# Delta-rule scan with forward and backward products in alternation, gathered in two bursts a step

## The chip, the cores and the metric

The kernel runs on one core of a Trainium2 chip. The metric is the device time of one execution in microseconds; the median of three runs before the change is 1783.05 us (1782.53 to 1787.27). The engines are named as the profile names them: PE (TensorE, with PEld for its weight loads), DVE (VectorE), ACT (ScalarE), POOL (GpSimd) and SP (SyncE, which here only issues DMAs).

## What is computed

One layer of an encoder on 1024 tokens of width 1024, all in fp32: a norm and a wide input projection; grouped attention; a gated delta rule that runs over the sequence forward and backward; gates and an output projection; then 16 experts that each choose 128 tokens. The change lies in the delta rule. With 8 heads of 64 and chunks of 64 tokens, each direction is a loop over 16 chunks (cut from the reference):

```python
def step(state, inp):
    u_n, w_n, a_n, qg_n, kd_n, gl_n = inp
    v_new = u_n - w_n @ state
    o_n = qg_n @ state + a_n @ v_new
    state = state * gl_n[..., None, None] + jnp.einsum('bhck,bhcv->bhkv', kd_n, v_new)
    return state, o_n
```

`w` and `u` hold the inverse of a 64x64 unit triangular matrix, one for each chunk, head and direction. `gl` is one decay a head and chunk, and `beta` and another decay scale the rows of `v_new`.

## The kernel before

Before the scan, the projections of q, k and v are normed and convolved (`dn_group`), the gates become scalars (`dn_gates`, `dn_scalars`), and `dn_tile` writes the masked products of each chunk to DRAM. `dn_invert` inverts only the two 32x32 blocks on the diagonal of each triangular matrix, on VectorE, and writes them to DRAM (`w_d`). The block beside the diagonal is made in the scan, by `scan_merge`: minus the product of the lower inverse, the block between them (`n_d`) and the upper inverse, as two rounds of 32x32 products, 8 heads for each direction.

The scan runs both directions at once. Step t works on chunk t forward and on chunk 15 - t backward. As t and 15 - t are one even and one odd, one chunk's 64 tokens lie on partitions 0 to 63 and the other's on 64 to 127 of the same tiles, and so in different row blocks of the PE array. A step consists of

- `pk` (L626): keys and queries times the state, 4 products of 128x128 for each direction; DVE scales them (L629) and takes them from v, which gives x (L633)
- `pv` (L638): the inverse times x, 8 products of 64x64 for each direction, all in one array block; DVE scales the result by the scalars `bs` to `vb` and `va` (L643, L644)
- `pu` (L653): the state's update, 8 products of 64x64 for each direction, whose outputs alternate between two column blocks; DVE adds it to the state, which was scaled by `gls` (L648, L655), and ACT copies the state into the form that `pk` reads (L658)
- `po` (L663): the output, 8 products of 64x64 for each direction, added into O (L669 to L672).

An fp32 product is two pairs of weight load and matmul, so a line with 8 products for each direction has 32 loads a step. `scan_merge` for step t + 1 (L604 to L613) has twice as many: 32 loads in its first round (L606), 32 in its second (L612). `scan_load` (L587 to L594) issues the ten DMAs of the next step on SP's queue.

The scan leaves PE room, and `late_fill` puts the rest of the input projection there: 15 groups of 48 matmuls of 128x512 (L1147). `scan` writes the order down: so many fills between the parts of a step (`FILL`), pieces of the attention's preparation (`attn_prep`, in the first eight steps; its transposes are L143), pieces of the output's norm (`scan_post`) and of the modulation (`mod_step`, L901, L903). This written order is a priority and not the final one: a planner with a cost model goes through the program and gives each engine, one instruction at a time, the first one in written order whose inputs it expects to be ready. The engine's queues then keep that order. PSUM tiles come in three kinds: "pj" for the fills, and "dn" and "tr" with two buffers each.

The scalars `gls` (for each step and head) and `bs` (for each step, row and head) are put in the order of the steps before the scan, by 32 and 64 copies on POOL (L430, L452, L453). POOL's queue also issues the weight loads of the projection (L269).

Of the kernel before, what the change touches and what calls it, by code (L numbers as in the profile page):

```python
# [7 lines left out]
F = mybir.dt.float32  # L8
# [24 lines left out]
FILL = 12, 10, 4, 4, 8, 48  # L33
# [40 lines left out]
def rev(ap):  # L74

    *dims, (step, n) = [list(x) for x in ap.ap]
    return bass.AP(tensor=ap.tensor, offset=ap.offset + step * (n - 1), ap=dims + [[-step, n]])


class K:  # L80
# [274 lines left out]
    def dn_gates(self, ps):  # L355
# [71 lines left out]
        for t in range(16):  # L427
            for d in range(2):
                n = t if d == 0 else 15 - t
                nc.gpsimd.tensor_copy(gls[:, t, d * 4:d * 4 + 4], gl[:, n // 2, n % 2, d * 4:d * 4 + 4])  # L430
        self.eg, self.gls, self.dk = eg, gls, dk

    def dn_scalars(self):
# [13 lines left out]
        for t in range(16):  # L447
            for d in range(2):
                n = t if d == 0 else 15 - t
                j, x = divmod(n, 2)  # L450
                rows = slice(64 * x, 64 * x + 64)
                nc.gpsimd.tensor_copy(bs[rows, t, 0, :], b2[rows, j, d, :])  # L452
                nc.gpsimd.tensor_copy(bs[rows, t, 1, :], b2d[rows, j, d, :])  # L453
# [119 lines left out]
    def scan_load(self, t):  # L573


        nc = self.nc
# [3 lines left out]
        for d in range(2):  # L580
            n = t if d == 0 else 15 - t
            x = n % 2
            r = slice(64 * x, 64 * x + 64)
            src = self.w_d[d].rearrange("(n h) (b s c) -> n b s h c", h=8, b=2, s=32)
            nsrc = self.n_d[d, n].rearrange("h (b s) (e c) -> b s h e c", b=2, e=2)
# [3 lines left out]
            nc.sync.dma_start(nf[f], nsrc[d, :, :, 1 - d, :])  # L589
            quads.append((f, o, slice(32 * d, 32 * d + 32), slice(32 - 32 * d, 64 - 32 * d)))  # L590
            nc.sync.dma_start(at[r].rearrange("p h c -> p (h c)"), self.a_d[d, n // 2, r])
            nc.sync.dma_start(kv[r], self.kv_d[n // 2, r])
            k = self.kqs[d][:, t % 2]
            nc.sync.dma_start(k, self.kq_d[n])  # L594
            kq.append(k)
        return w, at, kv, kq, nf, quads

    def scan_merge(self, ops):
# [4 lines left out]
        for f, o, cf, co in quads:  # L603
            nc.vector.transpose(wt[f], w[f, :, cf])  # L604
            for h in range(8):
                nc.tensor.matmul(pq[o, h], nf[f, h], wt[f, h], start=True, stop=True, skip_group_check=True)  # L606
            nc.scalar.activation(pt[o], pq[o], AF.Copy, scale=-1.0)
        yield
        pr = self.pa.tile([128, 8, 32], F, name="tr", bufs=2)
        for f, o, cf, co in quads:  # L610
            for h in range(8):
                nc.tensor.matmul(pr[f, h], pt[o, h], w[o, h, co], start=True, stop=True, skip_group_check=True)  # L612
            nc.scalar.copy(w[f, :, co], pr[f])  # L613

    def scan_step(self, t, ops):
# [20 lines left out]
        for r in rs:  # L636
            for h in range(8):
                nc.tensor.matmul(pv[r, h], w[r, h], x[r, h], start=True, stop=True, skip_group_check=True)  # L638
# [20 lines left out]
        yield  # L659
        po = self.pa.tile([128, 8, 64], F, name="dn", bufs=2)  # L660
        for d in range(2):
            for h in range(8):
# [250 lines left out]
    def scan(self, late, ak, sta):  # L913
# [23 lines left out]
        fill(FILL[5])  # L937
        for _ in self.scan_merge(ops):
            fill(6)
        for t in range(16):  # L940
            nxt = self.scan_load(t + 1) if t < 15 else None
            step = self.scan_step(t, ops)
            next(step)
            for _ in cur:
                pass
# [18 lines left out]
            fill(FILL[4])  # L964
# [660 lines left out]
```

## Time and profile before

| | |
|---|---|
| median of three runs | 1783.05 us |
| the profiled execution | 1782.9 us |
| its span (first to last instruction) | 1780.7 us |
| mean granted TensorE clock | 0.965 of full |
| PE busy | 1663.8 us (93%) |
| DVE busy | 1453.2 us (82%) |
| ACT busy | 924.4 us (52%) |
| POOL busy | 256.7 us (14%) |

Busy times are unions of an engine's instructions over the span; for PE the ends of matmuls are modelled and overlap, so weight loads (PEld) show its pace better. The scan's first state product stands at 412.8 us and its last at 747.0 us. Several small tiles share a buffer and stand under its name: the n blocks (`nf`) and their partner `wt` under Sc, and x, `va`, `vb` under st. In a group of the profile, the number behind the bar is the busy time, then the mean of one instruction, then the idle time of the engine just before them and what ended it.

### The profile page before, as it was taken

To read this page: it belongs to the slowest core of one execution; us is meant where nothing else is said; L and a number is where in the kernel's file an instruction comes from. 1 tells how busy PE (TensorE), PEld (TensorE's weight loads), DVE (VectorE), ACT (ScalarE), POOL (GpSimd) and SP (SyncE) were. 2 spreads that over 40 slices of the span, in tenths; PEclk is the share of its full clock that TensorE was granted. 3 is DMA by queue.
4 is the path that set the end of the run, shared out by engine and by line. 5 is a ranking of instruction groups with operands and counts; after the bars stand their busy time and mean duration, and the time that the engine had idled before them with its cause. 6 is when DMAs were issued, how large, how long until landed. Compare 5 with 4: busy or idle time off the path is not lost. (4 is left out here: it accounts for less than half of the span.)

```text
span 1780.7 us, 28660 instructions
## 1 busy us (share of the span) xinstructions
PE 1663.8 (93%) x10363; PEld 1333.4 (75%) x10363; DVE 1453.2 (82%) x2523; ACT 924.4 (52%) x1372; POOL 256.7 (14%) x287
## 2 busy tenths in 40 slices
PE   6999998389999999999999999939999999999997
PEld 4777876377887778778887778827777777777776
DVE  6899895965777667679998366889999999999997
ACT  5654522113332422268884133327777777777775
POOL 0041512021111100021111212220000110010000
PEclk8999999699999999899999999969999999999999
DMA  9466389256667775431114454569999999999991
GB/s 272 124 178 178 108 214 212 71 174 166 192 188 180 206 224 134 137 124 34 34 35 160 159 204 155 191 238 309 387 387 383 370 384 385 382 373 379 387 335 24
DMA packets 283053, 390.81 MB, mean 219 GB/s; under 512 B 78299, under 2 KB 151695, under 8 KB 282655
## 3 DMA queue, kind: packets, MB, share of 16 engines
q1 hardware_dynamic: 247103, 328.15, 55.5%
q0 software_dynamic: 12960, 47.19, 9.7%
q10 hardware_dynamic: 22848, 13.63, 2.7%
q8 instruction: 82, 1.34, 0.3%
q14 instruction: 60, 0.49, 0.1%
HBM read 330.14 MB, written 58.77 MB: 218 GB/s over the span
## 5 line engine op out<-in xcount | busy, mean ns | idle before, releaser
L1514 DVE TENSOR_TENSOR ew<-er,ew 128x1024 fp32r<-128x1024 f32 x384 | 452.2, 1219 | 30.1 <-ACT ew L1513 30.1
L1513 ACT CAST ew<-er 128x1024 fp32r<-128x1024 f32 x384 | 391.1, 1049 | 138.2 <-PE pj L1567 103.0
L1567 PE MATMUL pj<-ew,xT 128*128 128x512 f32 x1536 | 368.0, 396 | 4.5 <-DVE ew L1514 4.5
L1567 PEld LDWEIGHTS pj<-ew,xT 128*128 128x128 f32 x1536 | 283.3, 188 | 76.4 <-DVE ew L1514 19.5
L1584 PE MATMUL tr<-ew,aT 128*128 128x512 f32 x768 | 191.3, 398 | 0.0
L1584 PEld LDWEIGHTS tr<-ew,aT 128*128 128x128 f32 x768 | 139.7, 188 | 30.5 <-DVE ew L1514 3.5
L279 PE MATMUL pj<-hTh,wl 128*128 128x512 f32 (+1 forms) x368 | 118.6, 401 | 26.4 <-DVE wl L273 26.4
L279 PE MATMUL pj<-hTh,wh 128*128 128x512 f32 (+1 forms) x368 | 118.5, 402 | 3.6 <-ACT hTh L252 1.8
L279 PE MATMUL pj<-hTl,wh 128*128 128x512 f32 (+1 forms) x368 | 118.6, 399 | 1.4 <-DVE hTl L255 1.4
L272 ACT CAST wh<-wraw 128x1024 fp32r<-128x1024 f32 (+1 forms) x45 | 46.7, 1037 | 137.3 <-PE pj L279 66.5
L279 PEld LDWEIGHTS pj<-hTh,wl 128*128 128x128 f32 (+1 forms) x368 | 69.3, 189 | 43.5 <-DVE wl L273 27.0
L1590 POOL DMA_INDIRECT out_dram<-xe,idxT x16 | 37.1, 2317 | 405.6 <-DVE tok L1488 351.1
L269 POOL DMA_DIRECT2D wraw<-in_w_in_dram x42 | 37.7, 898 | 369.4 <-DVE wl L273 278.7
L834 DVE TENSOR_REDUCE am<-pj 128x1 f32<-128x1024 f32 x64 | 77.8, 1217 | 12.4 <-PE pj L829 11.8
L1193 PE MATMUL pj<-hTh,uw 128*128 128x512 f32 x256 | 83.5, 404 | 1.0 <-DVE uth L1199 0.5
L279 PEld LDWEIGHTS pj<-hTh,wh 128*128 128x128 f32 (+1 forms) x368 | 68.6, 190 | 19.8 <-ACT hTh L252 1.9
L1147 PE MATMUL pj<-hTh,wh 128*128 128x512 f32 x240 | 82.7, 412 | 0.0
L1147 PE MATMUL pj<-hTh,wl 128*128 128x512 f32 x240 | 81.9, 410 | 0.0
L279 PEld LDWEIGHTS pj<-hTl,wh 128*128 128x128 f32 (+1 forms) x368 | 68.7, 188 | 17.6 <-DVE hTl L255 2.0
L1147 PE MATMUL pj<-hTl,wh 128*128 128x512 f32 x240 | 81.3, 409 | 0.0
L836 ACT ACTIVATE ap<-pj,am 128x1024 f32<-128x1024 f32 x64 | 71.9, 1123 | 13.9 <-DVE am L834 8.5
L829 PE MATMUL pj<-kT,qT 128*128 128x512 f32 x256 | 77.0, 412 | 1.5 <-ACT ap L836 1.5
(373 smaller groups left out, 3144.5 us busy)
## 6 DMA issues: line engine op xcount, KB each, us to landing
er<-in_w_gate_dram SPq DMA_DIRECT2D x128, 512.0 KB, 7.2
er<-in_w_up_dram SPq DMA_DIRECT2D x128, 512.0 KB
er<-in_w_down_dram SPq DMA_DIRECT2D x128, 512.0 KB, 10.0
wraw<-in_w_in_dram POOLq DMA_DIRECT2D x42, 512.0 KB, 5.8
mw<-in_w_ada_dram SPq DMA_DIRECT2D x64, 256.0 KB, 3.6
wt<-in_w_ada_dram SPq DMA_DIRECT2D x16, 512.0 KB, 8.6
gate_d<-y ACTq DMA_DIRECT2D x32, 256.0 KB, 3.3
kv<-kv_d SPq DMA_DIRECT2D x32, 256.0 KB, 3.6
```

The lines of the kernel that those rows point to most:

```text
L269: (queue or nc.gpsimd).dma_start(raw[:, :, :n], self.i["w_in"][0, :, col:col + n].rearrange("(k p) c -> p k c", p=128))
L272: nc.scalar.copy(wh[:, :, :n], raw[:, :, :n])
L279: self.nc.tensor.matmul(ps[q][:n], w[:, k, :n], x[k][:, q * 512:(q + 1) * 512], start=(k == 0 and w is wh and x is self.hTh), stop=(k == 7 ...
L829: nc.tensor.matmul(ps[:, kh], qT[:, i * 128:(i + 1) * 128], self.kT[a][:, s, kh * 512:(kh + 1) * 512], start=(s == 0), stop=(s == 1), skip ...
L834: nc.vector.reduce_max(m, ps, axis=AX.X, negate=True)
L836: nc.scalar.activation(p, ps, AF.Exp, bias=m, scale=1.0, accum_out=self.rv[:, h, half * 4 + i:half * 4 + i + 1])
L1147: nc.tensor.matmul(ps[q], a[:, k], x[k][:, q * 512:(q + 1) * 512], start=(k == 0 and a is wh and x is self.hTh), stop=(k == 7 and a is wl))
L1193: nc.tensor.matmul(ps, w[:, k], v[k][:, qs], start=(k == 0 and p == 0), stop=(k == 3 and p == 2))
L1513: nc.scalar.copy(hi, raw)
L1514: nc.vector.tensor_sub(lo, raw, hi.bitcast(F))
L1567: nc.tensor.matmul(pg[m], x[:, 2 * kp + k], wi[:, k], start=(kp == 0 and k == 0 and n == 0), stop=(kp == 3 and k == 1 and n == 2))
L1584: nc.tensor.matmul(py[q], x[:, k], wi[:, q], start=(k == 0 and n == 0), stop=(k == 7 and n == 2))
```

## The change

Six edits, all of order but the last:

1. In `scan_merge`, `pv`, `pu` and `po` the loop over heads is now the outer one and that over directions the inner, so that successive products belong to different directions. In `pu` each direction has a tile of its own, one "dn" and one "tr".
2. In `scan_merge` the evacuations of a round (L607, L613) come behind the products of both directions.
3. `scan_step` loses a yield: `pu` and `po` are written as one piece.
4. In `scan` the next step's merge starts before `pv`, and its second round follows `po`. The fills between are 12, 10, 8 and 8, where they were 12, 10, 4, 4 and 8.
5. `scan_load` issues the W and n blocks of both directions first, then kqs, kv and sa.
6. `gls` is filled by 2 copies on ACT and `bs` by 8, with strides over the steps and, for the backward direction, a negative one (`rev1`).

```diff
-FILL = 12, 10, 4, 4, 8, 48
+FILL = 12, 10, 8, 8, 48
...
+def rev1(ap):
+    part, (step, n), *dims = [list(x) for x in ap.ap]
+    return bass.AP(tensor=ap.tensor, offset=ap.offset + step * (n - 1), ap=[part, [-step, n], *dims])
...
-        for t in range(16):
-            for d in range(2):
-                n = t if d == 0 else 15 - t
-                nc.gpsimd.tensor_copy(gls[:, t, d * 4:d * 4 + 4], gl[:, n // 2, n % 2, d * 4:d * 4 + 4])
+        gl = gl.rearrange("p j x e -> p (j x) e")
+        for d, turn in ((0, lambda a: a), (1, rev1)):
+            nc.scalar.copy(gls[:, :, d * 4:d * 4 + 4], turn(gl[:, :, d * 4:d * 4 + 4]))
...
-                nc.gpsimd.tensor_copy(bs[rows, t, 0, :], b2[rows, j, d, :])
-                nc.gpsimd.tensor_copy(bs[rows, t, 1, :], b2d[rows, j, d, :])
+        for x in range(2):
+            rows = slice(64 * x, 64 * x + 64)
+            for s, b in enumerate((b2, b2d)):
+                nc.scalar.copy(bs[rows, x::2, s, :], b[rows, :, 0, :])
+                nc.scalar.copy(bs[rows, 1 - x::2, s, :], rev1(b[rows, :, 1, :]))
...
             nc.vector.transpose(wt[f], w[f, :, cf])
-            for h in range(8):
+        for h in range(8):
+            for f, o, cf, co in quads:
                 nc.tensor.matmul(pq[o, h], nf[f, h], wt[f, h], start=True, stop=True, skip_group_check=True)
+        for f, o, cf, co in quads:
             nc.scalar.activation(pt[o], pq[o], AF.Copy, scale=-1.0)
...
-        for r in rs:
-            for h in range(8):
+        for h in range(8):
+            for r in rs:
                 nc.tensor.matmul(pv[r, h], w[r, h], x[r, h], start=True, stop=True, skip_group_check=True)
...
-            for d, r in enumerate(rs):
-                pu = self.pa.tile([128, 4, 64], F, name="dn", bufs=2)
-                for h in range(8):
-                    hb = 64 * (h % 2)
-                    nc.tensor.matmul(pu[hb:hb + 64, h // 2], kv[r, 0, h * 64:h * 64 + 64], vb[r, h],
+            pu = [self.pa.tile([128, 4, 64], F, name=n, bufs=2) for n in ("dn", "tr")]
+            for h in range(8):
+                hr = slice(64 * (h % 2), 64 * (h % 2) + 64)
+                for d, r in enumerate(rs):
+                    nc.tensor.matmul(pu[d][hr, h // 2], kv[r, 0, h * 64:h * 64 + 64], vb[r, h],
                                      start=True, stop=True, skip_group_check=True)
-                nc.vector.tensor_add(self.Sc[:, d * 4:d * 4 + 4], sg[:, d * 4:d * 4 + 4], pu)
+            for d in range(2):
+                nc.vector.tensor_add(self.Sc[:, d * 4:d * 4 + 4], sg[:, d * 4:d * 4 + 4], pu[d])
...
-        yield
         po = self.pa.tile([128, 8, 64], F, name="dn", bufs=2)
-        for d in range(2):
-            for h in range(8):
+        for h in range(8):
+            for d in range(2):
                 nc.tensor.matmul(po[os[d], h], at[rs[d], h], va[rs[d], h], start=True, stop=True,
...
             fill(FILL[0])
+            next(merge, None)
             next(step)
             fill(FILL[1])
             some(1)
-            next(step)
+            next(step, None)
+            next(merge, None)
             fill(FILL[2])
-            next(step, None)
-            merge = self.scan_merge(nxt) if nxt else iter(())
-            next(merge, None)
+            some(1)
             fill(FILL[3])
-            next(merge, None)
-            some(1)
-            fill(FILL[4])
```

## Rows read from the trace of the kernel before

**Rows 1.** Windows: busy us (instructions) of each engine, clock, DMA share, GB/s.

```profile
413.00:601.00 188.00, 182.63 (x1882) 149.38 (x1881) 135.84 (x327) 64.99 (x136) 23.32 (x36) 0.99 0.70 184
601.00:747.00 146.00, 142.54 (x1579) 115.15 (x1578) 100.26 (x221) 40.49 (x86) 6.85 (x7) 0.99 0.63 170
sum 334.00, PE 325.17 PEld 264.53 DVE 236.10 ACT 105.48 POOL 30.17; mean PE 162.59 PEld 132.27 DVE 118.05 ACT 52.74 POOL 15.09
```

**Rows 2.** Groups of weight loads, 413 to 747 us: busy, mean, idle before.

```profile
L1147 PEld LDWEIGHTS pj<-hTh,wl 128*128 128x128 f32 x205 | 37.8, 189 | 7.8 <-issue 0.2
...
L638 PEld LDWEIGHTS dn<-st,W 64*64 64x64 f32 x480 | 29.7, 134 | 7.9 <-issue 5.5 <-DVE ass L738 0.4 <-ACT pt L607 0.4
L663 PEld LDWEIGHTS dn<-st,sa 64*64 64x64 f32 x480 | 26.4, 134 | 2.5 <-issue 1.4 <-DVE Sc L655 0.4 <-DVE ra_y L116 0.4
L606 PEld LDWEIGHTS tr<-Sc 32*32 32x32 f32 x496 | 18.6, 110 | 7.0 <-issue 4.4 <-DVE Sc L604 1.4 <-DVE st L629 0.4
L612 PEld LDWEIGHTS tr<-W,pt 32*32 32x32 f32 x480 | 17.6, 109 | 5.2 <-ACT pt L607 1.8 <-ACT W L613 1.5 <-issue 1.4
L653 PEld LDWEIGHTS dn<-st,kv 64*64 64x64 f32 x480 | 15.1, 134 | 8.0 <-issue 4.0 <-DVE st L643 1.1 <-DVE ra_y L116 0.4
```

**Rows 3.** Timeline of weight loads in one step: start us, us, what, [idle before <-releaser].

```profile
707.37 0.57 PEld L606 LDWEIGHTS tr<-Sc 32*32 32x32 f32 x16 [0.17 <-issue]
...
708.86 0.57 PEld L606 LDWEIGHTS tr<-Sc 32*32 32x32 f32 x16
...
709.89 0.57 PEld L612 LDWEIGHTS tr<-W,pt 32*32 32x32 f32 x16
...
711.39 0.58 PEld L612 LDWEIGHTS tr<-W,pt 32*32 32x32 f32 x16 [0.36 <-ACT W L613]
712.01 1.00 PEld L638 LDWEIGHTS dn<-st,W 64*64 64x64 f32 x16
...
714.59 1.00 PEld L638 LDWEIGHTS dn<-st,W 64*64 64x64 f32 x16 [0.37 <-ACT pt L607]
...
716.95 0.84 PEld L653 LDWEIGHTS dn<-st,kv 64*64 64x64 f32 x32 [0.37 <-issue]
...
718.28 1.76 PEld L663 LDWEIGHTS dn<-st,sa 64*64 64x64 f32 x32 [0.24 <-DVE Sc L655]
```

**Rows 4.** Timeline, weight loads of the chunk products in `dn_tile`.

```profile
219.30 0.88 PEld L478 LDWEIGHTS dn<-kq 64*64 64x64 f32 x44 [0.17 <-issue]
```

**Rows 5.** Timeline of weight loads where L606 and L612 touch.

```profile
580.82 0.11 PEld L612 LDWEIGHTS tr<-W,pt 32*32 32x32 f32 x1
580.82 0.11 PEld L606 LDWEIGHTS tr<-Sc 32*32 32x32 f32 x1
```

**Rows 6.** Groups of DVE, 413 to 747 us.

```profile
L633 DVE TENSOR_TENSOR st<-kv,st 64x512 f32<-64x512 f32 x31 | 22.8, 736 | 0.6
L629 DVE TENSOR_TENSOR st<-dn,eg 128x512 f32<-128x512 f32 x31 | 21.4, 690 | 29.6 <-PE dn L626 29.3
```

**Rows 7.** Timeline of POOL and ACT around the scalar copies.

```profile
96.83 9.82 POOL L430 COPY gls<-ga 128x4 f32<-128x4 f32 x16
106.59 0.88 POOL L269 DMA_DIRECT2D wraw<-in_w_in_dram  x1
...
214.47 11.24 POOL L453 COPY bs<-b2d 64x8 f32<-64x8 f32 x32
225.65 1.76 POOL L269 DMA_DIRECT2D wraw<-in_w_in_dram  x2
...
205.22 1.06 ACT L313 ACTIVATE th<-y 128x1024 f32<-128x1024 f32 x1 [6.04 <-DVE y L311]
...
223.36 0.24 ACT L436 COPY ssqs<-ssq 64x64 f32<-64x64 f32 x1
```

**Rows 8.** DMA issues (KB, median us to landing) and a wait, 400 to 760 us.

```profile
W<-w_d SPq DMA_DIRECT2D x64, 32.0 KB, 3.4
...
Sc<-n_d SPq DMA_DIRECT2D x32, 32.0 KB, 11.5
...
DVE Sc L604 <- DMA W<-w_d: 3.0, 3, 1.4
```

More of the change, by code (lines that the diff above doesn't have):

```diff
@@ L446, in dn_scalars @@
         bs = self.ab.tile([128, 16, 2, 8], F, name="bs")
-        for t in range(16):
-            for d in range(2):
-                n = t if d == 0 else 15 - t
-                j, x = divmod(n, 2)
-                rows = slice(64 * x, 64 * x + 64)
-                nc.gpsimd.tensor_copy(bs[rows, t, 0, :], b2[rows, j, d, :])
-                nc.gpsimd.tensor_copy(bs[rows, t, 1, :], b2d[rows, j, d, :])
+        for x in range(2):
[3 more added lines that the diff above has]
+                nc.scalar.copy(bs[rows, 1 - x::2, s, :], rev1(b[rows, :, 1, :]))
         self.bs = bs
@@ L579, in scan_load @@
         kq, quads = [], []
-        for d in range(2):
-            n = t if d == 0 else 15 - t
+        ns = (t, 15 - t)
+        for d, n in enumerate(ns):
             x = n % 2
-            r = slice(64 * x, 64 * x + 64)
             src = self.w_d[d].rearrange("(n h) (b s c) -> n b s h c", h=8, b=2, s=32)
-            nsrc = self.n_d[d, n].rearrange("h (b s) (e c) -> b s h e c", b=2, e=2)
+            nsrc = self.n_d[d, n].rearrange("h (b s) (e c) -> b s h e c", b=2, e=2)[d, :, :, 1 - d, :]
             for b in range(2):
@@ L588, in scan_load @@
             f, o = slice(64 * x + 32 * d, 64 * x + 32 * d + 32), slice(64 * x + 32 - 32 * d, 64 * x + 64 - 32 * d)
-            nc.sync.dma_start(nf[f], nsrc[d, :, :, 1 - d, :])
+            nc.sync.dma_start(nf[f], nsrc)
             quads.append((f, o, slice(32 * d, 32 * d + 32), slice(32 - 32 * d, 64 - 32 * d)))
-            nc.sync.dma_start(at[r].rearrange("p h c -> p (h c)"), self.a_d[d, n // 2, r])
-            nc.sync.dma_start(kv[r], self.kv_d[n // 2, r])
+        for d, n in enumerate(ns):
+            r = slice(64 * (n % 2), 64 * (n % 2) + 64)
             k = self.kqs[d][:, t % 2]
@@ L595, in scan_load @@
             kq.append(k)
+            nc.sync.dma_start(kv[r], self.kv_d[n // 2, r])
+            nc.sync.dma_start(at[r].rearrange("p h c -> p (h c)"), self.a_d[d, n // 2, r])
         return w, at, kv, kq, nf, quads
@@ L609, in scan_merge @@
         pr = self.pa.tile([128, 8, 32], F, name="tr", bufs=2)
+        for h in range(8):
+            for f, o, cf, co in quads:
+                nc.tensor.matmul(pr[f, h], pt[o, h], w[o, h, co], start=True, stop=True, skip_group_check=True)
         for f, o, cf, co in quads:
-            for h in range(8):
-                nc.tensor.matmul(pr[f, h], pt[o, h], w[o, h, co], start=True, stop=True, skip_group_check=True)
             nc.scalar.copy(w[f, :, co], pr[f])
@@ L658, in scan_step @@
                     nc.scalar.copy(self.St[hr, d, :, hr], self.Sc[hr, d * 4:d * 4 + 4])
-        yield
         po = self.pa.tile([128, 8, 64], F, name="dn", bufs=2)
-        for d in range(2):
-            for h in range(8):
+        for h in range(8):
+            for d in range(2):
                 nc.tensor.matmul(po[os[d], h], at[rs[d], h], va[rs[d], h], start=True, stop=True,
@@ L936, in scan @@
         next(prep)
-        fill(FILL[5])
+        fill(FILL[4])
         for _ in self.scan_merge(ops):
@@ L943, in scan @@
             next(step)
+            merge = self.scan_merge(nxt) if nxt else iter(())
             for _ in cur:
```

## The prediction

> **What bounds the kernel now.** I first split the span by stage with the view of windows. The change touches the scan and two short runs of scalar copies before it. [...] VectorE is busy 135.8 of 188 (72%) and 100.3 of 146 us (69%). [...] A step takes 334/15 = 22.3 us. Busy does not mean well used, however: the groups of weight loads [rows 2] show what fills the step. Beside the projection work L1147 (the 720 "fill" matmuls, whose number doesn't change) stand five lines of small products, L606, L612, L638, L653, L663, with 480 or so loads each, 64x64 or 32x32 blocks of the array, and each has several us of idle time ahead of it.
>
> **How the small products run.** The timeline of the weight loads [rows 3] gives their pace. Sixteen loads of L638, all in one block of the array, take 1.00 us with the last load's 0.13 in it, so 58 ns from one to the next. Thirty-two of L653, which alternate between two column blocks, take 0.84 us: 0.71/31, 23 ns each, over twice the pace. L663, first 16 of one direction and then 16 of the other, takes 1.76 us; at 58 ns throughout it would be 31 x 0.058 + 0.13 = 1.93. The missing 0.17 us is three intervals: at the seam, where the two directions meet, pairs run side by side. This is the best evidence in the trace for the change, because the seam is just what alternation makes of the whole burst: another row block, another column block, the same PSUM tile. L478, which walks through four blocks, reaches 0.88/44 = 20 ns [rows 4], so two starts per 58 ns meet no issue limit. For the 32x32 blocks, where two bursts happen to touch, a load of L612 and one of L606 start together at 580.82 [rows 5], against one per 0.57/16 = 34 ns (32 without the tail) inside a burst [rows 3].
>
> **The change part by part.**
>
> *Alternation.* Per step: L638 32 x 0.058 = 1.86 us becomes 16 x 0.058 = 0.93, saves 0.93. L663 1.76 - 0.13 + 0.06 = 1.69 becomes 0.93, saves 0.76. L653 already uses two column blocks; with both directions four blocks are open: 0.84 - 0.13 + 0.06 = 0.77 becomes 8 x 0.058 = 0.46, saves 0.31 (bounds 0, if 23 ns is its floor, and 0.31). L606 and L612, 32 loads each at 32 ns, 1.02 each, become 0.51 each: 1.0 together (bounds 0 and 1.0, only the touching bursts speak for it). Sum 3.00 us a step. Some of this overlap exists already where the planner lets bursts touch, so I take 2.75, and for 15.5 steps (the last step has no L653, the first merge stands before the loop) 43 us. From below: only L638 and L663, where the seam shows it, 1.69 x 15.5 = 26 us. From above 46 (3.00 x 15.5).
>
> *Two bursts.* Each time the array goes from full to small blocks, a load waits until the running matmuls are through: 0.36 or 0.37 us idle at 711.39, 714.59 and 716.95 [rows 3], of which 0.04 is there between any two fills. In the 13 us from 707.37 to 720 this happens seven times (L606, L606, L612, L612 with L638 behind it, L638, L653, L663). Over 15 steps the idle time ahead of the five lines is 7.9 + 2.5 + 7.0 + 5.2 + 8.0 = 30.6 us [rows 2], 2.0 us a step. The new order writes the merge's first products ahead of L638 and its second ones behind L663, with fills outside. Two entries a step would cost 0.6 us. But the order on TensorE is the planner's, which lets in whatever is ready, and a burst whose input is late is split by fills, as L638's two halves are now. I take 3.5 entries of 0.28, and 0.2 for two changes between 32 and 64 blocks: 1.2 instead of 2.0, saves 0.8 x 15.5 = 13 us. Bounds 0 (as scattered as now) and 22 us (two entries).
>
> [...]
>
> *New waits.* L638 now waits for both directions' x before its first product, where the first direction could start alone. The x chain on VectorE is two times 0.69 + 0.74 us behind L626 [rows 6], the first pair beside L626's second half; 12 fills of (37.8 + 7.8)/205 = 0.22 us [rows 2] stand before it, 2.7 us. The two St copies and Sc sums that open the next step come behind both halves of L653, 0.2 us later than now for the first direction; 16 fills (3.5 us) and L663 cover them. Each cover is only just long enough, and behind a waiting small product all fills are stuck, for the queue is in order. VectorE already waits 29.3 us on L626 alone [rows 6]; when TensorE is quicker these waits shrink, and VectorE's share rises. With 236.1 us of work [rows 1] and a stage of 334 - 56 = 278 us it would be 85%. Two engines that hand work to each other lose some of this: I take 8 us of new idle time on TensorE (bounds 0 and 41; the latter if VectorE gets no further than 74%, just above its 72% of today: 236.1/0.74 = 319 us). I stay near the lower end, as VectorE's idle time is mostly waiting that shrinks.
>
> *Loads.* The ten DMAs of a step are the same; the W and n blocks go ahead of the rest on SP's queue, and no longer behind the first direction's sa, which waits for the last L663. The merge was already run in mid-step, ahead of L638 (707.37 against 712.01), so it isn't needed sooner. L604 lost 3.0 us in all on W [rows 8]. I take 0. The order of kqs before kv and sa costs nothing as sa is last needed.
>
> *Scalar copies.* 96 copies leave GpSimd, where they took 9.8 us for the last 16 of gls and 11.2 for the second 32 of bs; a weight load is issued right behind each (106.59, 225.65) [rows 7]. 10 copies come to ScalarE, 10 x 0.24 us by the nearest one, L436 = 2.4 us; it has a gap of 6.0 us before 205.22, just after the scalars are ready. Without that gap the 2.4 us would delay the conv chain. Nothing else waits for gls or bs until the scan. The earlier weight loads could help: I take 0, bounds -5 and +3 us.
>
> **Sum.** The profiled execution took 1782.9 us (span 1780.7), 0.15 under the median, so it stands for it. 1782.9 - 43 - 13 + 8 = 1734.9: forecast 1735 us, own range 1720 to 1750.
>
> **The rivals.**
> 1. *VectorE and the chain of a step take most of it.* For: 85% is needed, and the first half has the higher share; fills can be pulled ahead only while there are any. Against: VectorE's idle time now is mostly waiting for TensorE. At 78% the stage takes 236.1/0.78 = 303 us, 31 less than now: 1752; at 74% it takes 319: 1768. I put this case between, at 1758.
> [...]
> 3. *Nothing is lost again:* two entries a step, no new idle time: 1783 - 46 - 22 = 1715.
> 4. *Slower: late blocks in front of the chain.* On TensorE the merge's products are queued ahead of L638. If W or n lands after TensorE gets there, the whole queue stops, and with it the step. n took 11.5 us to land in the one case that is shown, W 3.4 [rows 8], and a quicker step means more traffic in each us (DMA share 0.70 and 0.63 now [rows 1]). From 56/15 = 3.7 us of such stops a step the change loses; at 5 us it is 1783 - 56 + 15 x 5 = 1802. Against: only 3.0 us are lost on W in all now, and the blocks leave earlier.
> 5. *It does not do what it says:* the planner splits the bursts by direction again, since they are ordered one instruction at a time: within 5 us of before.
>
> **How the numbers follow.** Forecast 0.52, rival 1 0.23, rival 2 0.08, rival 3 0.08, rival 4 0.05, rival 5 0.04. The range 1712 to 1770 takes in the first four but for their tails and leaves out about 0.16. A change of 0.3% (5.3 us) is about what a measurement of this kernel tells from none. Faster: 0.52 + 0.23 + 0.08 + 0.08 = 0.91, of which the tail of rival 2 takes 0.01: 0.90; same 0.04 (that tail and most of rival 5); slower 0.06 (rival 4 and a hundredth of 5).
>
> **What would show it.** Right: L638 and L663 32 loads in about 1.0 us, L653 in 0.6, L606 and L612 in 0.65; the idle time ahead of the five lines half of 30.6; the scan from L626 to L626 about 286 us for 15 steps; everything behind it shifted as a block. Wrong: pace still 58 ns in alternation (rival 2), long waits of L638 or L653 on VectorE (rival 1), of L604 or L606 on DMA (rival 4), or a lower granted clock within the scan.

## The result and the profile after

The changed kernel took 1737.19 us (median of 4 runs, 1736.07 to 1737.44) against 1784.09 us for the kernel before on the same chip: a ratio of 0.9734, 95% interval 0.9717 to 0.9751. The forecast was 1735. The profiled execution has a span of 1733.9 us against 1780.7, 46.8 us less. Cut at the first and the last load of pk and at the reductions of the attention scores, it lies here:

| stretch | before, us | after, us | difference |
|---|---|---|---|
| start to first pk | 412.8 | 407.6 | -5.2 |
| first to last pk (scan) | 334.2 | 302.3 | -31.9 |
| last pk to first score reduction | 5.5 | -0.9 | -6.4 |
| first to last score reduction | 193.8 | 191.1 | -2.7 |
| from there to the end | 834.4 | 833.8 | -0.6 |

So the total came out as forecast, but the scan did not: it was to lose 48 us and lost 32, or 38 with its tail. A minus sign in the third row says that the first score reduction starts ahead of the last pk. Each cut is of one profiled execution, and executions of the kernel before lie between 1774.0 and 1790.0 us, so a difference of a few us between two cuts shows little by itself. Names in the new numbering: L633 is pk, L611 pq, L618 pr, L645 pv, L660 pu, L670 po, L608 the W transposes, L636 and L640 the x chain, L1152 the fills.

Windows of the changed kernel, the scan from its first to its last pk and then its two halves; columns as in [rows 1]:

```profile
407.00:710.00 303.00, 291.48 (x3499) 231.50 (x3492) 239.41 (x547) 106.55 (x226) 30.68 (x44) 0.98 0.75 197
...
408.00:565.00 157.00, 149.78 (x1730) 120.05 (x1729) 124.83 (x290) 59.97 (x128) 22.49 (x35) 0.98 0.77 199
565.00:710.00 145.00, 140.70 (x1748) 110.58 (x1748) 114.45 (x256) 46.00 (x98) 7.73 (x8) 0.97 0.73 196
```

TensorE is busy 291.5 of 303 us with work that took 325.2 of 334 [rows 1]. VectorE's 239.4 us of work is now 79% of the stretch (71% before), and TensorE stands 11.5 us in it (8.8 before).

Groups of weight loads of the changed kernel in the scan (407 to 711 us): busy us, mean ns of one, idle us ahead of them; they answer to [rows 2].

```profile
L1152 PEld LDWEIGHTS pj<-hTh,wl 128*128 128x128 f32 x206 | 37.9, 189 | 7.6
...
L645 PEld LDWEIGHTS dn<-st,W 64*64 64x64 f32 x482 | 18.9, 140 | 11.9 <-issue 9.1 <-PE dn L633 0.6 <-DVE ra_y L122 0.4
L670 PEld LDWEIGHTS dn<-st,sa 64*64 64x64 f32 x480 | 16.2, 134 | 3.5 <-issue 3.4
L611 PEld LDWEIGHTS tr<-Sc 32*32 32x32 f32 x494 | 9.8, 107 | 6.8 <-issue 2.3 <-DVE xnq L752 2.2 <-DVE Sc L608 0.7
L618 PEld LDWEIGHTS tr<-W,pt 32*32 32x32 f32 x512 | 9.7, 107 | 3.7 <-issue 2.5 <-ACT pt L613 0.4
L660 PEld LDWEIGHTS dn<-st,kv 64*64 64x64 f32 x240 | 8.5, 134 | 7.0 <-DVE st L650 2.9 <-issue 2.5 <-DVE ra_y L122 0.4
L660 PEld LDWEIGHTS tr<-st,kv 64*64 64x64 f32 x240 | 8.2, 134 | 1.7 <-issue 1.6
```

Overlapping loads are counted once as busy: four groups take half to two thirds of what they took, though a single load still lasts 107 ns (32x32) or 134 to 140 ns (64x64). pu does not: 8.5 + 8.2 = 16.7 against 15.1. And the idle time ahead of the five is not halved: 11.9 + 3.5 + 6.8 + 3.7 + 8.7 = 34.6 us against 30.6.

Two stretches of the timeline of weight loads of the changed kernel, 586 to 594 us and 648 to 663 us, fills left out:

```profile
586.77 0.58 PEld L611 LDWEIGHTS tr<-Sc 32*32 32x32 f32 x32
587.40 0.19 PEld L645 LDWEIGHTS dn<-st,W 64*64 64x64 f32 x2
588.78 1.00 PEld L645 LDWEIGHTS dn<-st,W 64*64 64x64 f32 x30 [0.37 <-issue]
591.89 0.13 PEld L660 LDWEIGHTS dn<-st,kv 64*64 64x64 f32 x1 [0.35 <-issue]
591.90 0.13 PEld L660 LDWEIGHTS tr<-st,kv 64*64 64x64 f32 x1
...
592.31 0.14 PEld L660 LDWEIGHTS tr<-st,kv 64*64 64x64 f32 x1
592.36 1.02 PEld L670 LDWEIGHTS dn<-st,sa 64*64 64x64 f32 x32
593.44 0.58 PEld L618 LDWEIGHTS tr<-W,pt 32*32 32x32 f32 x32
...
648.00 0.54 PEld L660 LDWEIGHTS dn<-st,kv 64*64 64x64 f32 x16 [0.36 <-DVE st L650]
649.74 0.89 PEld L670 LDWEIGHTS dn<-st,sa 64*64 64x64 f32 x28 [0.36 <-issue]
650.71 0.13 PEld L611 LDWEIGHTS tr<-Sc 32*32 32x32 f32 x2
650.88 0.43 PEld L660 LDWEIGHTS tr<-st,kv 64*64 64x64 f32 x12
...
653.64 0.57 PEld L611 LDWEIGHTS tr<-Sc 32*32 32x32 f32 x30 [0.35 <-issue]
655.96 0.58 PEld L618 LDWEIGHTS tr<-W,pt 32*32 32x32 f32 x30
662.93 1.00 PEld L645 LDWEIGHTS dn<-st,W 64*64 64x64 f32 x30 [0.35 <-issue]
```

L645 and L670 now do 32 loads in the 1.0 us that 16 took [rows 3], L611 and L618 32 in the 0.58 that 16 took. The second burst of the first stretch is as the code is written: pu's forward ("dn") and backward ("tr") products in turn, 32 loads in 0.55 us, then po and pr without a fill between. It is the exception. In 14 of the 15 steps that have pu, its directions run apart, as at 648.00 and 650.88 (in one of the 14 a few of the last loads alternate), and fills stand between the products of one burst.

For one number per kernel I took, in the stretch from first to last pk, the time from each weight load's start to the next one's. "Small" is the sum of these where both are small products, "entries" the number (and sum) of those from any other load, nearly always a 128x128 one, to a small one. For the kernel before, small is 25.7 (pv) + 24.2 (po) + 15.3 (pq) + 14.4 (pr) + 12.1 (pu) = 91.7 us; after, 14.4 + 14.1 + 8.1 + 7.7 + 12.3 = 56.6. That is 35.1 us less, more than the 31.9 that the stretch lost: entries gave 3.3 back, and all other intervals came out 0.1 lower. An interval holds the idle time in it, so these sums and the idle time overlap.

| kernel | first pk | first to last pk, us | small, us | entries (us) | PE idle, us | median, us |
|---|---|---|---|---|---|---|
| before | 412.8 | 334.2 | 91.7 | 109 (48.7) | 8.8 | 1784.1 |
| after | 407.6 | 302.3 | 56.6 | 100 (52.0) | 11.5 | 1737.2 |
| alternation alone | 416.8 | 300.1 | 54.4 | 106 (51.4) | 10.9 | 1741.3 |
| pv and po alone | 412.3 | 312.3 | 70.0 | 110 (48.9) | 7.0 | 1757.4 |
| pq and pr alone | 414.2 | 316.2 | 77.4 | 109 (48.6) | 6.1 | 1759.7 |
| after without alternation | 412.5 | 328.0 | 93.1 | 116 (51.8) | 0.9 | 1779.1 |
| placement alone | 413.9 | 344.5 | 97.0 | 120 (56.5) | 4.4 | 1774.1 |
| bursts in written order | 411.2 | 299.3 | 60.6 | 47 (31.4) | 28.2 | 1742.6 |
| pu in written order | 410.7 | 299.5 | 56.5 | 90 (51.4) | 13.6 | 1733.2 |
| loads alone | 414.2 | 328.4 | 91.1 | 105 (47.6) | 2.6 | 1767.6 |
| after, old load order | 411.6 | 313.1 | 56.2 | 107 (62.5) | 16.8 | 1744.3 |

Medians come from five sessions, in which the kernel before had medians of 1781.3 to 1784.1; the ratios below are each to the kernel before of their own session.

### The profile page after: what moved, and what is told of

The parts are those of the page before. It is cut to its first block, busy times and chain, and to the rows that moved or that the text cites. A ratio compares the mean times of both kernels' runs of the same rounds, so it can differ in the third digit from the quotient of the medians.

```text
span 1733.9 us, 28593 instructions
## 1 busy us (share of the span) xinstructions
PE 1615.1 (93%) x10363; PEld 1287.0 (74%) x10363; DVE 1454.2 (84%) x2523; ACT 924.5 (53%) x1382; POOL 211.9 (12%) x191
## 5 line engine op out<-in xcount | busy, mean ns | idle before, releaser
L841 DVE TENSOR_REDUCE am<-pj 128x1 f32<-128x1024 f32 x64 | 77.8, 1218 | 10.6 <-PE pj L836 10.0
L1152 PE MATMUL pj<-hTh,wh 128*128 128x512 f32 x240 | 82.9, 416 | 0.6 <-ACT y L1157 0.4
L1152 PE MATMUL pj<-hTl,wh 128*128 128x512 f32 x240 | 82.1, 411 | 0.0
L1152 PE MATMUL pj<-hTh,wl 128*128 128x512 f32 x240 | 82.1, 410 | 0.0
```

Of the source, the lines that this page charges most:

```text
L841: nc.vector.reduce_max(m, ps, axis=AX.X, negate=True)
L1152: nc.tensor.matmul(ps[q], a[:, k], x[k][:, q * 512:(q + 1) * 512], start=(k == 0 and a is wh and x is self.hTh), stop=(k == 7 and a is wl))
```

## The experiments

Each part of the change was first put alone on the kernel before.

**Alternation alone.**

```
-            for h in range(8):            # under "for f, o, cf, co in quads:"
-                nc.tensor.matmul(pq[o, h], ...)
+        for h in range(8):
+            for f, o, cf, co in quads:
+                nc.tensor.matmul(pq[o, h], ...)
(pr, pv, pu, po likewise; a round's copies behind both directions, pu's second tile a "tr")
```

> Kernel before with edits 1 and 2 alone: the two directions' products in alternation (the two merge rounds, pv, pu with its two tiles, po), written places, fills, loads and copies as before. Pace theory: the time comes from small products running side by side; the trace of the changed kernel shows L638, L663, L606 and L612 shorter by 10.7, 10.5, 7.1 and 7.0 us over 15 steps, so about 35 us: 1745 to 1755 us. Placement theory (the written order with two bursts is what pays): within 12 us of before, 1771 or more.

Measured 1741.3 us, ratio 0.9771 (0.9740 to 0.9801). Small products fell by 37 us, the stretch by 34. The pace theory holds, with 4 us more than its range gave, and the placement theory falls. Alternation alone gives 41 us of the 47, so nearly all of the gain is in this one exchange of loops.

**Placement alone** (two bursts a step, the new fills).

```
-FILL = 12, 10, 4, 4, 8, 48
+FILL = 12, 10, 8, 8, 48
+            next(merge, None)      # pq ahead of pv
             next(step)
...
+            next(merge, None)      # pr behind po
```

> Kernel before with edits 3 and 4 alone: merge ahead of pv and behind po, one yield less, fills 12, 10, 8, 8; products by direction as before. Pace theory: the changed trace still enters small blocks 6 times a step (7 before), so placement is worth little: 1776 to 1786 us. Placement theory, and my prediction's second term (13 us, up to 22): 1761 to 1770 us.

Ratio 0.9954 (0.9939 to 0.9970), a gain of 8 us: 1774.05 us lies between the two theories' ranges. But entries rose from 109 to 120. (The profiled execution, with a span of 1783.6 us, was the longest of this kernel, so its stretch of 344.5 us says little.) Whatever gained, it is not fewer entries.

**Scalar copies alone.**

```
-        for t in range(16):
-            for d in range(2):
-                n = t if d == 0 else 15 - t
-                nc.gpsimd.tensor_copy(gls[:, t, d * 4:d * 4 + 4], ...)
+        for d, turn in ((0, lambda a: a), (1, rev1)):
+            nc.scalar.copy(gls[:, :, d * 4:d * 4 + 4], turn(...))
(bs likewise)
```

> Kernel before with edit 6 alone: gls and bs by 10 copies on ScalarE in place of 96 on GpSimd. The changed trace is 4 us ahead of before from 111 us on, with VectorE busy 29.4 of 30 us between 80 and 110 us where it was 27.5. If the copies do that: 1778 to 1780 us. My prediction had 0 (bounds -5 and +3): 1783 us, and the 4 us would then be from the planner's other order.

1779.56 us, ratio 0.9987 (0.9969 to 1.0005): not told from nothing. The scan's first pk came at 409.3 us for 412.8.

**Loads alone.**

```
-            nc.sync.dma_start(at[r]..., self.a_d[d, n // 2, r])   # per direction, behind W and n
-            nc.sync.dma_start(kv[r], self.kv_d[n // 2, r])
+        for d, n in enumerate(ns):                                 # W and n of both directions first
+            nc.sync.dma_start(k, self.kq_d[n]); ... kv ... at
```

> Kernel before with edit 5 alone: W and n blocks first, then kqs, kv, sa. Prediction: 0, so 1780 to 1786 us. Rival: the merge was held by its loads, and the earlier W and n pay by themselves: 1775 us or less.

Ratio 0.9919 (0.9889 to 0.9949), 14.5 us faster. I had put this edit at zero. PE's idle time in the stretch fell from 8.8 to 2.6 us, and the 3.2 us stand of pk for VectorE that the kernel before shows at 542 us is gone, as is the stand of 2.9 us ahead of the last step's transposes. VectorE's waits for W fell as well, but just from 3.0 us [rows 8] to 0.4, so they are not the 14.5. Of the 10.4 us by which the profiled executions differ, 5.8 lie between first and last pk and 7.5 between there and the first score reduction, while the first pk came 1.4 later. What gives the gain in this kernel stays open.

The four gains add up to 41 + 8 + 2 + 14.5, about 66 us; the change gives 47. So the parts don't add, and parts were then taken out of the changed kernel instead.

**The changed kernel without alternation.** The edit is the first one's reverse.

> The changed kernel with its first part undone: the products pq, pr, pv, pu and po go one direction after the other again; the two bursts, the order of the loads and the scalar copies stay as changed. Nothing is left out of the computation. Theory A (pace: alternating products keep two blocks of the array busy at once, and that is most of the gain, whatever the rest does): the start-to-start intervals of the five groups go from 56.6 us back to about 92 us, the stretch from the first pk to the last from 302 to 330-340 us, time 1767-1777 us (1737 + 35, less a few us that DVE hides). Theory B (the parts add up: the other three alone gave 8.3, 2.4 and 14.5 us): 1783 - 25 = 1758 us. Theory C (most of the gain is that the last step of the scan no longer runs dry, so that the granted clock stays at 1.00 behind it): no more than 10 us back, 1740-1747 us. A falls if the intervals return to 92 us and the time stays under 1755.

1779.09 us, ratio 0.9972 (0.9949 to 0.9996), just above the range of A. The small products return to 93.1 us and the time nearly to that of before: alternation is worth 42 us here too, and the other three parts together 5. B (1758) falls, and with it the thought that all parts share the missing 19 us: alternation is worth the same without the others (41) as on top of them (42), while placement, copies and loads, 8, 2 and 14.5 us alone, give 5 together. It is these three that don't add. C falls too. Two groups of this kernel, 407 to 760 us, with pv at L642 and po at L666, have their busy time of [rows 2] back (29.7 and 26.4 there, for 480 records each):

```profile
L642 PEld LDWEIGHTS dn<-st,W 64*64 64x64 f32 x512 | 31.4, 134 | 7.4 <-issue 4.6 <-PE dn L630 0.7 <-DVE st L637 0.4
L666 PEld LDWEIGHTS dn<-st,sa 64*64 64x64 f32 x512 | 29.6, 140 | 3.5 <-issue 1.3 <-DVE Sc L659 0.9 <-DVE ra_y L118 0.4
```

**Half of the alternation at a time**, on the kernel before: pv and po, then pq and pr; the edits are two of the four hunks each.

> The kernel before with only pv and po (64x64) alternating between the two directions; pq, pr and pu, the placement, the loads and the scalar copies stay as before. Nothing is left out. Theory A (pace: one block of the array takes about 55 ns a load, two in turn 28 ns each): the intervals of pv and po fall from 25.7 + 24.2 to about 28 us, pq, pr and pu stay at 15, 14 and 12 us; the stretch from first to last pk falls by about 21 us, time 1757-1765 us. Theory B (the gain hangs on a threshold elsewhere, in the granted clock or in the planner's order, and isn't a sum over products): either under 10 us (1774 or more) or as much as all five together (1741-1748 us).

> The kernel before with only pq and pr (32x32) alternating between the two directions; pv, po and pu, the placement, the loads and the scalar copies stay as before. Nothing is left out. Theory A (pace: 32 ns a load in one block, 16 ns in two): the intervals of pq and pr fall from 15.3 + 14.4 to about 15 us, pv and po stay at 25 us each; time 14 us below before, 1764-1773 us. Theory B (not a sum over products): no change (1778-1784 us), or as much as all five together (1741-1748 us).

pv and po: 1757.36 us, ratio 0.9864 (0.9819 to 0.9908). pq and pr: 1759.68 us, ratio 0.9872 (0.9825 to 0.9919). The first is as A had it, in its stretch (-21.9 us) and in its groups (28.3 us for 49.9). The second moved the groups as A had it (15.9 for 29.7) and the time further, by 22 for 14 us, below A's range; the stretch lost 18. Together 46 against 41 for all five at once: within the intervals a sum over products, not a threshold. The groups of the two kernels, 407 to 760 us, pv and po being L638 and L663 in the first and L641 and L666 in the second, pq and pr L606 and L612, then L607 and L614:

```profile
L638 PEld LDWEIGHTS dn<-st,W 64*64 64x64 f32 x512 | 20.3, 139 | 8.2 <-issue 5.3 <-DVE st L633 0.4 <-DVE ass L738 0.4
L606 PEld LDWEIGHTS tr<-Sc 32*32 32x32 f32 x512 | 18.5, 107 | 7.8 <-issue 4.4 <-DVE Sc L604 1.8 <-ACT pt L607 0.7
L612 PEld LDWEIGHTS tr<-W,pt 32*32 32x32 f32 x512 | 18.5, 107 | 5.6 <-ACT pt L607 2.2 <-ACT W L613 1.3 <-issue 1.3
L663 PEld LDWEIGHTS dn<-st,sa 64*64 64x64 f32 x512 | 17.7, 137 | 3.0 <-issue 1.8 <-DVE Sc L655 0.4 <-DVE ro_a L115 0.4
```

```profile
L641 PEld LDWEIGHTS dn<-st,W 64*64 64x64 f32 x512 | 32.2, 137 | 8.7 <-issue 5.9 <-ACT W L616 1.2 <-ACT y L1155 0.4
L666 PEld LDWEIGHTS dn<-st,sa 64*64 64x64 f32 x512 | 28.3, 134 | 2.3 <-issue 1.1 <-DVE st L647 0.4 <-DVE ro_y L116 0.4
L614 PEld LDWEIGHTS tr<-W,pt 32*32 32x32 f32 x512 | 11.0, 108 | 7.0 <-ACT pt L609 3.6 <-issue 2.2 <-ACT y L1155 0.2
L607 PEld LDWEIGHTS tr<-Sc 32*32 32x32 f32 x512 | 9.9, 107 | 4.4 <-issue 2.2 <-DVE Sc L604 1.8 <-DMA W<-w_d 0.2
```

Only what alternates shrinks. Between these two kernels, at 512 loads each, it is by 37% in pv and po and by 41 and 46% in pr and pq.

**The bursts in written order.**

```
-            next(merge, None)
-            next(step)
+            with self.tc.manual_schedule(engines={mybir.EngineType.PE}):
+                next(merge, None)
+                next(step)
(the second burst likewise)
```

> The changed kernel with the order on PE's queue kept as written in each of the two bursts of a step (other work may still come between, but the products of a burst keep their order). Nothing is left out. In the changed kernel the planner split the bursts: 100 entries from full 128x128 loads into small blocks, and in 14 of 15 steps pu's two directions went one behind the other (8 products, then 8), with intervals of 6 and 50 ns in turn; in the one step where they alternated, four blocks in turn, the intervals were 6, 7, 7 and 38 ns. Theory A (order): pu's intervals fall from 12.3 us to 7-8 us in sum, entries to 40-60, each worth about 0.3 us (52 us in 100 entries against 0.21 us between full loads), so 1737 - 5 - 12 to -18 = about 1717 us. Theory B (waiting): the fixed order makes PE stand while DVE finishes x, va and vb or the last 'tr' tile comes free, 0.5-2 us a step, 16 steps; PE idle in the stretch rises from 11.5 us to 20-40 us and eats the gain, 1730-1755 us. Theory C (pu is held by the two passes of each fp32 product, not by the order): pu stays at 25 ns a load, 12 us.

1742.56 us, ratio 0.9783 (0.9750 to 0.9816), and so not faster than the change itself. Entries fell from 100 to 47 and their time by 20.6 us, pu's intervals from 12.3 to 7.0 us: A is right on both, but not on its 1717 us. TensorE's idle time rose from 11.5 to 28.2 us, and the stretch is just 3.0 us shorter: B took the gain. Small products as a whole rose from 56.6 to 60.6 us, since waits within a burst stand in their intervals, as po's (20.4 for 14.1), behind which pr now waits. C is refuted: with both directions in turn pu runs at 14 ns a load, as in the 0.55 us of the first stretch above. Waits of TensorE in this kernel, 407 to 715 us (who waited for whom, us in total, times, longest):

```profile
PE tr L149 <- DVE st L696: 6.7, 3, 4.7
PE tr L611 <- issue: 5.5, 5, 3.5
PE tr L618 <- issue: 4.2, 3, 2.2
PE tr L149 <- DVE y L902: 3.1, 1, 3.1
```

The bursts' own products, pq (L611) and pr (L618), stand about as long in these lines, 9.7 us, as transposes that the planner put where they had to wait for VectorE, 9.8 us: those of the scan's output in the first line, with the longest stand, and of attention's preparation in the last. All of the queue stands behind either, for up to 3.5 us behind pq and 4.7 us behind a transpose.

**Only pu in written order.**

```
+            with self.tc.manual_schedule(engines={mybir.EngineType.PE}):
             for h in range(8):
                 ...
                     nc.tensor.matmul(pu[d][hr, h // 2], ...)
```

> The changed kernel with only the 16 products pu of a step kept in written order on PE's queue, so that forward and backward alternate over four blocks. Nothing is left out. Theory A (order): mean interval of pu from 25 to about 14 ns, 12.3 us to 6.5-7.5 us in sum, time 1731-1735 us at most 6 us below the changed kernel's 1737. Theory B (waiting): the first product waits for both directions' vb and both tiles, and the state update, which the next step's pk wait for, comes later; the stretch from first to last pk stays 302 us or grows, 1735-1750 us. Theory C (two passes): pu stays at 25 ns.

1733.22 us, ratio 0.9731 (0.9694 to 0.9768): the same as the change's 0.9734. The time is in A's range, but cannot be told from no change. pu runs at about 14 ns a load where it alternates, and C is refuted here too, but its intervals fall just from 12.3 to 9.8 us, short of A's 7.5: in 13 of the 15 steps the first product, whose tile is a "dn", went ahead alone, and the next one, the first to write the "tr" tile, followed only behind other work. A waiting product keeps its place: pv's wait for x, once 3.1 us in the changed kernel, comes five times here (waits of TensorE, 407 to 715 us):

```profile
PE dn L645 <- DVE st L640: 4.0, 5, 1.2
```

**One filler fewer a step, in the kernel before.**

```
-FILL = 12, 10, 4, 4, 8, 48
+FILL = 12, 10, 4, 4, 7, 48
```

> The kernel before with one number changed: one filler product fewer behind the last stage of each scan step (7 for 8), which leaves 16 of them for the end of the scan. In the kernel before PE stands 2.88 us at 739.2 us for the last step's transposes with no filler left, and the granted clock is 0.78 in the 5 us after 740 us, 0.50 from 745 to 760 us and 0.67 in the next 5 us. Nothing is left out. Theory A (that stand costs its own time and, through the clock, about 8 us more): no stand over 1 us there, clock near 1.00 in that stretch, time 1772-1777 us. Theory B (the clock there costs nothing, since DVE and ACT set the pace behind the scan): clock 1.00, time 1780-1785 us. Theory C (one filler fewer a step opens new gaps in the steps): 1785-1795 us, PE idle in the scan up by 5 us or more.

1789.47 us, ratio 1.0037 (1.0019 to 1.0055). The question was whether the change gained by ending a stand: in the kernel before TensorE runs out of fillers in the last step and waits 2.5 us from 739.7 us for the transposes' input (2.9 us counted between weight loads), and the granted clock then falls: it is 0.50 from 743 to 760 us. Windows of the kernel before and of this one (columns as in [rows 1]):

```profile
735.00:740.00 5.00, 4.66 (x30) 3.58 (x28) 4.44 (x12) 0.75 (x2) 0.00 (x0) 1.00 0.35 106
740.00:745.00 5.00, 2.88 (x26) 2.62 (x26) 3.32 (x9) 0.82 (x2) 0.00 (x0) 0.78 0.39 130
745.00:760.00 15.00, 15.00 (x121) 12.03 (x120) 4.68 (x6) 3.90 (x8) 0.00 (x0) 0.50 0.67 203
```

```profile
601.00:750.00 149.00, 143.42 (x1575) 117.53 (x1575) 100.31 (x225) 41.15 (x86) 6.80 (x7) 0.93 0.62 168
740.00:765.00 25.00, 24.03 (x206) 19.57 (x204) 15.35 (x37) 7.23 (x15) 0.00 (x0) 0.94 0.50 154
```

From 740 to 765 us the stand is gone and the clock is at 0.94, and yet the kernel is 7 us slower: the second half of the scan lost clock instead (0.93 for 0.99 in [rows 1]) and the scan took 2.6 us more; from the last pk to the first score reduction it took 8.8 us for 5.5, and 15 weight loads of left-over fillers stand there, where the kernel before has none. A is refuted as a gain of its own. C has the time right, but not its sign: idle time in the stretch rose by 1.6 us, not 5. What the stand costs by itself stays open.

**The changed kernel with the old load order, and with the old copies.** The edits are the reverse of the third and fourth above.

> The changed kernel with the order of the step's loads undone (each direction's W/n, at, kv and kq one after the other, as before). Nothing is left out. Theory A (the loads land long before they are used, and what the reordering gave alone, 14.5 us, is the planner's other order around it: one stand of 3.2 us for DVE that is gone and a half clock that fell elsewhere): within 5 us of the changed kernel, 1732-1742 us. Theory B (the order of the loads itself is worth 14 us): 1747-1755 us, with waits for DMA in the scan of 5 us or more in sum (in the kernel before 1.7 us in one place).

> The changed kernel with the per-step scalars copied as before, by 32 + 64 small copies on GpSimd in place of 10 strided ones on ScalarE. Nothing is left out. Theory A (what ends the preparation is not these copies): within 4 us of the changed kernel, 1734-1741 us, the scan's first pk 0-3 us later. Theory B (the 5.1 us by which the scan starts earlier in the changed kernel come from them): 1740-1744 us, first pk at 411-413 us for 407.6.

Old load order: 1744.34 us, ratio 0.9787 (0.9757 to 0.9816), 0.5% above the change's 0.9734. Between the two theories: the order is worth about 9 us by the ratios, 7 by the medians. Rows of this kernel, 405 to 745 us (waits of TensorE, then of VectorE in its transposes of W; the last is the changed kernel's) and 411 to 725 us (group):

```profile
PE tr L610 <- DVE xnq L751: 6.4, 2, 3.8
...
PE tr L610 <- DMA Sc<-n_d: 2.5, 1, 2.5
...
DVE Sc L607 <- DMA W<-w_d: 7.3, 4, 3.6
...
DVE Sc L608 <- DMA W<-w_d: 0.8, 2, 0.5
```

```profile
L610 PEld LDWEIGHTS tr<-Sc 32*32 32x32 f32 x510 | 11.3, 110 | 17.4 <-issue 7.2 <-DVE xnq L751 3.7 <-DVE O L677 2.9
```

pq (L610) has 17.4 us of idle time ahead of it, against 6.8 (L611) in the changed kernel. One stand of 2.5 us ends with the landing of n itself; two of together 6.4 us end with VectorE, when it has read a "tr" tile of attention's preparation (xnq). In both cases VectorE had itself stood for W just before, 3.6 us until 511.6 and 2.5 us until 563.1, and the reading of the tile came 3.8 and 1.6 us after that in its queue. So B's 5 us of waiting for DMA are there, but on VectorE: 7.3 us for W, where the changed kernel has 0.8. A run that parts n from W was not made.

Old copies: 1737.14 us, ratio 0.9757 (0.9724 to 0.9789) against 0.9734: not told apart. The first pk came 4.1 us later (411.7), as B had it, but the stretch was 6.2 us shorter and the time is A's.

## Why the prediction was right, point by point

**The total: right, and its closeness luck.** The forecast was -48 us, all in the scan, with everything behind it shifted as a block; measured were -46.8, of which -31.9 in the scan and -14.9 ahead of it and behind it, where the sum had no term. In the scan itself the sum missed by 16 us: alternation came 8 us short and the entries 16, while the new waits were 5 less (idle time is part of all three, so they don't add up exactly). Of the signs that were named, pv, po, pq and pr came, but not pu, not half of the 30.6 us of idle time, and not a scan of 286 us.

**Alternation (43 us): right in its mechanism, 8 us too large in size.** By the intervals, pv gave 11.3 us for 14.4 (0.93 x 15.5), po 10.1 for 11.8, pq and pr 13.9 for 15.5: 35 where these four had 42. Two blocks in turn take 27 to 30 ns a load in 64x64 and 15 in 32x32, close to half of 58 and 31, and after the change the four take 44.3 us, just what the sum gave them (2.88 x 15.5 = 44.6). The difference lies before the change: there they took 79.6 us, where the sum had 5.59 x 15.5 = 86.6, since it counted a full interval for the last load of each burst, which no small load follows, and half a step more than lies between the first and the last pk.

pu gave nothing for 4.8 us. The step that failed is "with both directions four blocks are open". Its 23 ns before were no floor, which was the lower bound I gave: inside one direction they were about 28 ns already, and less where the two directions met. The planner ran the directions apart, rival 5 in one line of five; where they do alternate, a load takes 14 ns. Why it did so is not shown. What fits is the "tr" tile that the change gave to the backward half: of this kind there are two buffers, which pq, pr and transposes (L149) use as well, and in all 15 steps the backward products came only after the next step's pq had begun, as at 650.71 and 650.88. With alternation alone, where pq is written behind pu, 5 of the 15 steps alternate in full, and pu's intervals are 10.6 us. So placement took back some of what alternation gave. No run has two "dn" tiles.

The end-to-end price, 42 us when alternation is taken out of the changed kernel, meets the term of 43, but not for the term's reason alone. Of the 40.5 us between the two profiled executions just 25.7 lie between the first and the last pk: 36.5 us less of small products and 10.6 us more of idle time. The other 14.8 us lie ahead of the first pk (4.9) and behind the last, where few small products run, and are not explained.

**Two bursts (13 us): wrong.** Entries went from 109 to 100, not to 3.5 a step (54), and their time rose by 3.3 us. The warning in the text, that the planner lets in whatever is ready, was the case; the value should have been at the lower bound, 0. (0.8 x 15.5 is also 12.4, not 13.) When the order is forced, the entries do give 20 us, but TensorE waits 17 us more and the time is no shorter.

**New waits (8 us): the net is smaller, the term itself about right.** Idle time rose by 2.7 us against the kernel before. Against the changed kernel without alternation, which stands 0.9 us, it rose by 10.6: the other three parts ended the stands of before, and alternation brought new ones. The longest are one that was named, pv for x, and one that was not, a transpose of attention's preparation behind VectorE's state sum, which reads pu's "tr" tile (waits of TensorE, 405 to 745 us):

```profile
PE dn L645 <- DVE st L640: 3.1, 1, 3.1
PE tr L149 <- DVE Sc L663: 3.1, 1, 3.1
```

The fall of VectorE's wait for pk shows where the slack went; this row answers to L629 in [rows 6], where it was 29.3:

```profile
L636 DVE TENSOR_TENSOR st<-dn,eg 128x512 f32<-128x512 f32 x32 | 22.1, 689 | 10.9 <-PE dn L633 10.4
```

**Loads (0): wrong by 7 to 9 us.** I had argued from when TensorE needs W and n and from 3.0 us of VectorE's waiting for W. But W passes VectorE first, in order with everything else there, and at the changed kernel's pace the old order makes VectorE wait 7.3 us for W, the new one 0.8.

**Copies (0, bounds -5 and +3): within the bounds.** In the six kernels profiled with the new copies, the first pk stands at 407.6 to 412.5 us, 410.5 in the mean; in eight with the old ones at 411.7 to 416.8, 413.6 in the mean. That is 3 us of the 5.2 by which the scan starts earlier; the ranges overlap, and the time of the whole kernel doesn't show it.

**What I had not looked for:** the tail. From the last pk to the first score reduction the change took 6.4 us, where the kernel before runs at 0.50 of the clock and the changed one at 1.00. But the clock alone does not make it long: in the filler run the same cut takes 8.8 us, with 15 loads of fillers in it, at a clock of 1.00 (750 to 759 us). Alternation alone, placement alone and loads alone each bring it below zero (-7.3, -3.0 and -2.0 us), so what shortens it is not told apart.

**The rivals.** Rival 1 put the stage at 303 us with VectorE at 78%; it was 302 at 79%. The total was not its 1752 only because of the 14.9 us outside the scan. Its reason is not borne out as it stands: 303 us in place of 278 would be 25 us of new idle time on TensorE, and it was 2.7; the length came from terms that failed. But that VectorE and the chain of a step hold the stage there is not excluded: of the six kernels with all five products in alternation, five lie at 296 to 302 us, though the entries take 31 us in one of them and 52 in another, and no run takes work from VectorE. Rival 2 had a pace of 58 ns in alternation as its sign, and it fell: pv, po, pq and pr each write one tile from both directions and take 27 to 30 ns a load in 64x64, where one block takes 58, and 15 in 32x32 for 31. The two directions write different partitions of that tile; no run has them write the same ones. Rival 3 asked for what the run with the bursts in written order did: 47 entries, but not without loss. Rival 4 did not come: the waits of TensorE have 0.3 us for a DMA in all the scan, and that is for a fill.

## What to carry to other kernels

In these runs the small products of one 64x64 block followed one another at 58 ns a load, and exchanging two loops, so that neighbours use two blocks, brought that to 27 to 30 ns (in 32x32 from 31 to 15); look for such bursts, and price them from the intervals between weight loads, not from busy time. Before counting on a new order, see whether the scheduler keeps it, whether a buffer that two parts of the work share lets it, and whether a wait in an in-order queue gives back what the order saves (with the bursts in written order the entries took 20.6 us less, and TensorE stood 16.7 us more). Test the parts of a change by taking them out of the finished kernel as well as by adding them alone: here alternation is worth 41 us alone and 42 at the end, but the other three parts 25 alone and 5 together. And where a total comes out as forecast, see whether its stages do.

## What the runs showed of the hardware that was not expected

Four 64x64 blocks in turn took 14 ns a load (intervals 6, 7, 7 and 38 ns in turn, changed kernel, 591.9 to 592.3 us), two 27 to 30 ns (7 and 51 in turn, 592.4 to 593.2 us), one 58 ns (kernel before, [rows 3]): a round over the blocks took 58 ns in each of the three cases, and a load its share of that. It made little difference whether two blocks differ in rows and columns (pv 30, po 28 ns) or in columns alone (one direction of pu, 27 ns).

The granted clock fell to 0.50 in or just behind stands of TensorE (before, one of 3.2 us from 542.1 us, with a clock of 0.50 from 545 us, and one of 2.5 us from 739.7, with 0.50 from 743; in the changed kernel two of 3.1 us from 558.2 and 598.5, with 0.50 from 560 and 601), but not only there: in the changed kernel without alternation it fell in a stretch where TensorE was busy throughout, with no stand over 0.5 us in the scan ahead of it.

```profile
600.00:605.00 5.00, 5.00 (x86) 4.17 (x84) 0.43 (x1) 2.11 (x6) 0.00 (x0) 1.00 0.60 157
605.00:610.00 5.00, 5.00 (x75) 3.76 (x71) 1.95 (x4) 1.37 (x4) 0.00 (x0) 0.74 0.67 185
610.00:615.00 5.00, 5.00 (x50) 4.82 (x49) 2.25 (x4) 1.70 (x5) 0.00 (x0) 0.50 0.98 310
```

What set it off there is open. These stretches lie elsewhere in each kernel, and the lost clock is 5 to 17 us, 12.0 before and 6.9 after (the shortfall of the granted clock, summed over windows of 5 us from 400 to 780 us); this may be part of why the parts don't add, but no run separates it.
